# A hybrid two-layer model step: 48 instead of 32 latent tokens outside the dense expert products, 56 instead of 64 early blocks, index picks laid out anew

## The chip, the cores and the metric

The kernel runs on one core of a Trainium2 chip. Its engines work side by side, each through its own list of instructions in order: TensorE (PE; its weight loads are shown apart as PEld) multiplies matrices into PSUM, VectorE (DVE), ScalarE (ACT) and GpSimd (POOL) compute element by element, and SyncE (SP) issues transfers. The metric is the device time of one execution in microseconds (us); a time of a kernel is the median of several executions.

## The reference, cut to what matters

Two layers run over 640 tokens of 1024 features: 512 latent tokens and 128 context tokens. Each layer is a mixer (a gated convolution in layer 0, a state-space scan in layer 1) and then PEER, an expert layer with 16,384 experts of one neuron each. A token has 8 heads; each head scores two sets of 128 keys, keeps the top 16 of both, forms the sums, and keeps the best 16 pairs as experts:

```python
s1, i1 = lax.top_k(s[:, :, 0], PEER_TOPK)
s2, i2 = lax.top_k(s[:, :, 1], PEER_TOPK)
cand = (s1[..., :, None] + s2[..., None, :]).reshape(T, PEER_HEADS, PEER_TOPK * PEER_TOPK)
sc, pos = lax.top_k(cand, PEER_TOPK)
idx = jnp.take_along_axis(cidx, pos, axis=-1)
g = jax.nn.softmax(sc, axis=-1)
act = jnp.einsum('td,thkd->thk', tb, u[ib])
out = jnp.einsum('thk,thkd->td', jax.nn.gelu(act, approximate=False) * gb, v[ib])
```

So each token uses 128 of the experts: a dot product of the token with the expert's row of u, a GELU, a gate, and a weighted sum of rows of v.

## The kernel before, in words

PEER is computed in two ways. **Dense**: for `ND` = 480 latent tokens the kernel multiplies all 16,384 experts, in `NBLK` = 128 blocks of 128 experts. The first product (`u_blocks`, tile `pact`) takes a block's u against the tokens: 8 slices of features, each as three products (`mm3`, lines 125 to 127: high x high, low x high, high x low parts of a float32 number), 24 in all, each 128 x 128 weights against 480 columns. ScalarE applies GELU (tile `ga`). VectorE multiplies by the token's gates, which are zero for most experts (tile `h`, line 572), and splits the result into a high and a low part (line 581). The second product takes the block's v, again 8 x 3 products of 480 columns: six of eight feature slices sum up in PSUM (`acc`), two share a bank (`rot`) and are added to `sacc` by VectorE (line 641). Weights arrive as 512 KB tiles (`ur`, `wr`) on SP's queue; ScalarE makes their high part (line 89), VectorE the low part (`ul`, `wl`, line 98).

**Gathered**: the other 32 latent tokens (`NX`) and the 128 context tokens go another way. In a slot, GpSimd gathers one expert's row of u and v for each of 128 partitions (tile `uv`, 1 MB, three buffers, line 587), VectorE takes the dot with the token rows `hrow` (line 594), ScalarE applies GELU and the gate, and VectorE adds the weighted v row to `cacc` (line 604). The 32 latent tokens take four partitions each, so 32 slots serve them; 128 slots serve the context tokens, whose rows are loaded into `hrow` when the first group ends (`context_rows`). Then TensorE folds the four partial sums of a token with `quad` (`last_tokens`, line 616), into the bank `pact`.

Order in a layer: the norm also writes the token rows through TensorE transposes (`context_rows` in `peer_gates`); then come 16 key projections with scores, top-16 and `combine`, the picks of the second index, the gates spread to a table in DRAM by products of one-hot tiles (30 chunks of `TB` = 16 tokens, tile `pg`), and the main loop over the blocks. In the stages before the main loop, `fill` places steps of first products (three products, counted as 650 ns) between other work until `NSP` = 64 blocks are done; their activations wait in DRAM (`adram`). In the main loop the blocks that follow the early ones compute both products. `GATHER` says how many slots a block gets: 0.62 where it has only the second product, 1.95 where it has both. The order in the main loop is written out by hand; ahead of it a scheduler orders the instructions by their place in the code.

A pick (`pick`, lines 822 to 826) selects one of 16 values for each of 16 slots: a comparison makes a 16 x 16 mask (`cmp`), VectorE multiplies it with the values (line 825) and sums (line 826). It is done 8 times in `combine` (line 848) and 8 times in the pick stage (line 888) per layer.

Of the kernel before, what the change touches and what calls it, by code (L numbers as in the profile page):

```python
# [9 lines left out]
F32 = mybir.dt.float32  # L10
# [14 lines left out]
NX = 32  # L25
ND = NL - NX
NG = NX + P
KT = 8
# [4 lines left out]
NSP = 64  # L33
# [3 lines left out]
SG = 32  # L37
SW = 64
CH = 5
FILL_Q = (0, 9000)  # L40
GATHER = (0.62, 1.95)
# [5 lines left out]
FILL_T = 9000  # L47
FILL_G = 4800
# [65 lines left out]
class K:  # L114
# [28 lines left out]
    def run(s):  # L143
        nc, A = s.nc, s.A
        with ExitStack() as ctx:
# [9 lines left out]
            s.hdram = dram.tile([P, D], F32, name="hdram")  # L155
# [325 lines left out]
    def peer(s, i):  # L481
        nc, A = s.nc, s.A
        with ExitStack() as ctx:
# [52 lines left out]
            with ExitStack() as mc:  # L536
# [10 lines left out]
                xt = ap.tile([P, KT, NX], F32, name="xt")  # L547
                dg = ap.tile([P, NG], F32, name="dg")

                quad = ap.tile([P, NX], F32, name="quad")  # L550
                nc.vector.tensor_reduce(quad, s.ident.rearrange("p (q t) -> p t q", t=NX), axis=AX.X, op=ALU.add)
# [40 lines left out]
                def dot(n):  # L592
                    if n < NG:
                        nc.vector.scalar_tensor_tensor(UV[n][:, :D], UV[n][:, :D], 1.0, rows[n >= NX], op0=ALU.mult,  # L594
                                                       op1=ALU.mult, accum_out=dg[:, n:n + 1])
                        nc.scalar.activation(dg[:, n:n + 1], dg[:, n:n + 1], AF.Gelu)  # L596
                        nc.scalar.activation(dg[:, n:n + 1], dg[:, n:n + 1], AF.Copy, scale=cg[:, n:n + 1])

                def add_v(n):
                    t = UV.pop(n)  # L600
                    if n in (0, NX):
# [5 lines left out]
                def context_rows():  # L607

                    rows.append(hp.tile([P, D], F32, name="hrow"))
                    nc.sync.dma_start(rows[1], s.hdram)  # L610

                def last_tokens():

                    o = vps.tile([P, NL], F32, name="pact")[:, :KT * NX].rearrange("p (k t) -> p k t", t=NX)
                    for k in range(KT):
                        nc.tensor.matmul(o[:, k, :], cacc[:, k * P:(k + 1) * P], quad, start=True, stop=True)
                    nc.vector.tensor_tensor(xt, o, s.mod[i][:, 40:, 0:1].to_broadcast([P, KT, NX]), op=ALU.mult)
# [25 lines left out]
                for a in range(NBLK - 2):  # L643
# [27 lines left out]
                    while slot + due < NG and (credit >= 1 or a == NBLK - 3):  # L671
                        due, credit = due + 1, credit - 1
                    n0 = int(a + LAG >= NSP)
                    for n in range(max(due, 1)):
                        if n == 0 and n0 == 0:
                            add_rot(o, n6, a < 2)
                        if n < due:
# [4 lines left out]
                            if slot == NX - 1:  # L682
                                context_rows()
# [6 lines left out]
                    if before < NX <= slot:  # L690
                        assert a + LAG < NSP
                        last_tokens()
# [50 lines left out]
    def peer_gates(s, i, hi, lo, hrow, cidx, cgate, wq, fill, V, order):  # L743
        nc, A = s.nc, s.A
        with ExitStack() as pc:
# [6 lines left out]
            hctx = tk.tile([P, D], F32, name="hctx")  # L752
# [4 lines left out]
            def context_rows(k, t):  # L757

                if k % 4 == 0:
                    bank.append(qps.tile([P, 8, P], F32, name="pss", bufs=1))  # L760
                o = bank[-1]
                nc.tensor.transpose(o[:, k % 4, :], t[:, NL:], s.ident)
                four = tk.tile([P, P // NX, NX], F32, name="four", bufs=2)
                nc.gpsimd.tensor_copy(four, t[:, None, ND:NL].to_broadcast([P, P // NX, NX]))
                nc.tensor.transpose(o[:, 4 + k % 4, :], four.rearrange("p a b -> p (a b)"), s.ident)
                if k % 4 == 3:
                    for n, dst in ((0, hctx), (4, hrow)):
                        nc.scalar.activation(dst[:, (k - 3) * P:(k + 1) * P],
                                             o[:, n:n + 4].rearrange("p a b -> p (a b)"), AF.Copy)
                if k == KT - 1:  # L770
                    nc.scalar.dma_start(s.hdram, hctx)

            with ExitStack() as nx:
                s.norm(i, 1, hi, lo, s.pool(nx, "normtmp"), context_rows)
            s.close_x()

            stc = tk.tile([P, 16, 16], F16, name="stc")
            qc = tk.tile([P, 16, 16], F16, name="qc")
            for r in range(16):
                nc.gpsimd.memset(stc[:, r, :], float(STARTS[r]))  # L780
                nc.gpsimd.memset(qc[:, r, :], float(r))

            B16 = [P, CH, 16, 16]
            with qx:
# [37 lines left out]
                def pick(eq, vals, dst):  # L822

                    pr = qp.tile(B16, F16, name="pr")
                    nc.vector.tensor_tensor(pr, eq, vals[:, :, :, None].to_broadcast(B16), op=ALU.mult)  # L825
                    nc.vector.tensor_reduce(dst, pr.rearrange("p t r k -> p t k r"), axis=AX.X, op=ALU.add)

                def combine(h, a, b):
                    (v1, f1), (v2, _) = a, b
                    cd = qp.tile([P, CH, NCAND], F32, name="cd")  # L830
                    for p0, p1, nq, o in CAND:
# [9 lines left out]
                    pf = qp.tile([P, CH, 16], F16, name="pf")  # L841
                    nc.vector.tensor_copy(pf, pos)
# [4 lines left out]
                    cmp = qp.tile(B16, F16, name="cmp")  # L847
                    nc.vector.tensor_tensor(cmp, pf[:, :, None, :].to_broadcast(B16),
                                            stc[:, None].to_broadcast(B16), op=ALU.is_ge)
                    pick(cmp, d1, I1[:, :, h, :])  # L850
# [32 lines left out]
                for h in range(8):  # L883
                    fill(FILL_G)
                    q = qp.tile([P, CH, 16], F16, name="pf")
                    nc.vector.tensor_copy(q, PF[:, :, h, :])
                    eq = qp.tile(B16, F16, name="cmp")
                    nc.vector.tensor_tensor(eq, q[:, :, None, :].to_broadcast(B16),
# [562 lines left out]
```

## Time and profile before

| | us |
|---|---|
| median of three executions | 4118.25 (4109.04 to 4119.88) |
| the profiled execution | 4117.18 |
| its span in the trace | 4115.5 |
| TensorE busy | 4000.5 |
| VectorE busy | 3414.4 |
| ScalarE busy | 1661.4 |

The span runs from the first to the last instruction of the trace; the rest of the execution's time lies around it. Mean moved bytes are 233 GB/s over the span, and the mean granted clock of TensorE is 0.987 of full speed. In layer 0, PEER takes about 285 to 1866 us: scores to 492, picks to 586, one-hot chunks to 804, the rest of the early blocks to 846, blocks with the second product alone to 1163, blocks with both products to 1824, and the end. In layer 1 the same stages begin near 2524 us. A busy share is an average over stages, and an engine's idle time matters only where something waits for it.

### The profile page before, as it was taken

Reading aid. Unit: us, or ns where it says so; the run is one execution under the profiler, and the core shown is the slowest. Engines: PE = TensorE matmul, PEld = TensorE weight load, DVE = VectorE, ACT = ScalarE, POOL = GpSimd, SP = SyncE. Lnnn points to the kernel's source line nnn. Section 1 sums busy time; section 2 is a strip of 40 time slices with the busy share of each in tenths; the row PEclk is TensorE's granted clock in tenths of the full one; section 3 lists DMA queues with packets and bytes.
Section 4 is the critical chain, followed back from the end, with each engine's and each line's share of the span. In section 5 each row is a group of like instructions: output and inputs, shape, how many; then the busy total and the mean of one; then the engine's idle time right before and its main releaser. Section 6 shows DMA issues by size and latency. Waiting matters only on the chain.

```text
span 4115.5 us, 59000 instructions
## 1 busy us (share of the span) xinstructions
PE 4000.5 (97%) x22253; PEld 3543.9 (86%) x22253; DVE 3414.4 (83%) x6324; ACT 1661.4 (40%) x3060; POOL 421.6 (10%) x535
## 2 busy tenths in 40 slices
PE   8999999999999999999999999999999999999998
PEld 6999978788888888888999998987878888888887
DVE  7979997678788888878999867998858878888886
ACT  5233234433333333336555644223443333333332
POOL 0000000001111111111010100000001111111110
PEclk8999999999999999999999999999999999999999
DMA  6643238888888888963333234224888889998894
GB/s 218 219 159 109 81 131 248 266 307 321 313 316 324 322 322 322 327 249 123 118 102 119 85 128 148 94 86 161 249 280 300 323 316 325 323 323 321 323 324 181
DMA packets 344807, 957.33 MB, mean 233 GB/s; under 512 B 30091, under 2 KB 192139, under 8 KB 302537
## 3 DMA queue, kind: packets, MB, share of 16 engines
q1 hardware_dynamic: 147914, 514.53, 36.5%
q0 software_dynamic: 52224, 338.36, 22.1%
q10 hardware_dynamic: 144384, 100.67, 7.7%
q8 instruction: 174, 2.85, 0.3%
q14 instruction: 111, 0.91, 0.1%
HBM read 839.34 MB, written 114.04 MB: 232 GB/s over the span
## 4 chain that ended last, share of the span: by engine, by line
issue 41%; PE 32%; DVE 14%; POOL 8%; ACT 2%; DMA 2%; ACTq 1%; POOLq 0%; SPq 0%; DVEq 0%
POOL uv L587 8%; PE pact L125 3%; PE pact L126 3%; PE pact L127 3%; PE pj L125 2%; PE pj L126 2%; PE pj L127 2%; DVE ul L98 1%; DVE wl L98 1%; PE pg L978 1%; DMA uv<-uv,cidx 1%; PE pg L979 1%; DVE pr L825 1%; DVE idx L799 1%; DVE scr L795 1%
## 5 line engine op out<-in xcount | busy, mean ns | idle before, releaser
L125 PE MATMUL pact<-hnh,uh 128*128 128x480 f32 x2048 | 789.7, 386 | 12.7 <-ACT ga L508 9.4
L127 PE MATMUL pact<-hnh,ul 128*128 128x480 f32 x2048 | 781.7, 382 | 9.6 <-DVE ul L98 9.4
L126 PE MATMUL pact<-hnl,uh 128*128 128x480 f32 x2048 | 784.1, 383 | 0.0
L125 PE MATMUL acc<-h,wh 128*128 128x480 f32 x1536 | 584.6, 381 | 0.0
L127 PE MATMUL acc<-h,wl 128*128 128x480 f32 x1536 | 581.7, 379 | 0.0
L126 PE MATMUL acc<-h,wh 128*128 128x480 f32 x1536 | 581.7, 379 | 0.0
L89 ACT ACTIVATE wh<-wr 128x1024 fp32r<-128x1024 f32 x385 | 404.8, 1052 | 398.1 <-DMA wr<-uv 105.1
L98 DVE TENSOR_TENSOR wl<-wr,wh 128x1024 fp32r<-128x1024 f32 x385 | 469.7, 1220 | 59.4 <-ACT wh L89 58.3
L587 POOL DMA_INDIRECT uv<-uv,cidx x320 | 335.7, 1049 | 1661.8 <-DVE cacc L604 1540.1
L125 PEld LDWEIGHTS pact<-hnh,uh 128*128 128x128 f32 x2048 | 387.0, 189 | 76.1 <-ACT ga L508 13.1
L127 PEld LDWEIGHTS pact<-hnh,ul 128*128 128x128 f32 x2048 | 386.5, 189 | 74.0 <-DVE ul L98 13.6
L594 DVE SCALAR_TENSOR_TENSOR uv<-uv,hrow 128x1024 f32<-128x1024 f32 x320 | 390.8, 1221 | 57.3 <-DMA uv<-uv,cidx 55.6
L126 PEld LDWEIGHTS pact<-hnl,uh 128*128 128x128 f32 x2048 | 386.5, 189 | 58.3
L604 DVE SCALAR_TENSOR_TENSOR cacc<-uv,dg,cacc 128x1024 f32<-128x1024 f32 x316 | 405.1, 1282 | 0.0
L508 ACT ACTIVATE ga<-pact 128x480 f32<-128x480 f32 x256 | 145.6, 569 | 626.3 <-PE pact L127 626.0
L98 DVE TENSOR_TENSOR ul<-ur,uh 128x1024 fp32r<-128x1024 f32 x256 | 312.3, 1220 | 88.7 <-ACT uh L89 88.2
L89 ACT ACTIVATE uh<-ur 128x1024 fp32r<-128x1024 f32 x256 | 269.0, 1052 | 252.5 <-DMA ur<-uT 111.2
L581 DVE TENSOR_TENSOR h<-h,h 128x480 fp32r<-128x480 f32 x256 | 168.5, 658 | 197.0 <-PE rot L126 196.5
L127 PEld LDWEIGHTS acc<-h,wl 128*128 128x128 f32 x1536 | 289.1, 188 | 46.1
L126 PEld LDWEIGHTS acc<-h,wh 128*128 128x128 f32 x1536 | 289.1, 188 | 44.1
L125 PEld LDWEIGHTS acc<-h,wh 128*128 128x128 f32 x1536 | 289.4, 188 | 43.1
L596 ACT ACTIVATE dg<-dg 128x1 f32<-128x1 f32 x320 | 63.9, 200 | 422.3 <-DVE uv L594 422.3
(342 smaller groups left out, 8004.8 us busy)
## 6 DMA issues: line engine op xcount, KB each, us to landing
ur<-uT SPq DMA_DIRECT2D x256, 512.0 KB
wr<-uv SPq DMA_DIRECT2D x256, 512.0 KB
gdram<-st ACTq DMA_DIRECT2D x30, 2048.0 KB
gt<-gdram SPq DMA_DIRECT2D x62, 960.0 KB
mw<-ada_wT SPq DMA_DIRECT2D x80, 512.0 KB
adram<-ga ACTq DMA_DIRECT2D x128, 240.0 KB
ga<-adram SPq DMA_DIRECT2D x128, 240.0 KB
wr<-ssd_w SPq DMA_DIRECT2D x48, 512.0 KB
```

The lines of the kernel that those rows point to most:

```text
L89: s.K.nc.scalar.activation(hi.rearrange("p a b -> p (a b)"), s.raw[s.nh], AF.Copy)
L98: s.K.nc.vector.tensor_sub(lo.rearrange("p a b -> p (a b)"), s.raw.pop(s.ns), hi.rearrange("p a b -> p (a b)").bitcast(F32))
L125: mm(out, wh, mh, start=start, stop=False)
L126: mm(out, wh, ml, start=False, stop=False)
L127: mm(out, wl, mh, start=False, stop=stop)
L508: nc.scalar.activation(g, pa, AF.Gelu)
L581: nc.vector.tensor_sub(h2, h, h1.bitcast(F32))
L587: nc.gpsimd.indirect_dma_start(out=t[:], out_offset=None, in_=A["uv"].rearrange("l e d -> (l e) d"), in_offset=bass.IndirectOffsetOnAxis(a ...
L594: nc.vector.scalar_tensor_tensor(UV[n][:, :D], UV[n][:, :D], 1.0, rows[n >= NX], op0=ALU.mult, op1=ALU.mult, accum_out=dg[:, n:n + 1])
L596: nc.scalar.activation(dg[:, n:n + 1], dg[:, n:n + 1], AF.Gelu)
L604: nc.vector.scalar_tensor_tensor(cacc, t[:, D:], dg[:, n:n + 1], cacc, op0=ALU.mult, op1=ALU.add)
L795: nc.vector.match_replace(scr[:, t], v[:, t, :8], src[:, t], imm_value=-3e38)
```

## The change

`NX` becomes two groups, 16 and 32 tokens, so `ND` is 464: every dense product has 464 columns. The 16 tokens take eight partitions each, 16 slots; the layer has 176 slots instead of 160. `NSP` is 56. Token rows are made and loaded for three groups (two changes of `hrow` in the main loop, two foldings), and a block's slots do not run past a group's end. The picks compare pairs of neighbouring slots, with the values along the inner axis. The gate table is written in sub-chunks of 16 tokens, two to a transfer, and the last of the now 29 chunks alone. `FILL_Q`, `FILL_P` and `GATHER` set new amounts of fill and slots.

```diff
-NX = 32
-ND = NL - NX
-NG = NX + P
+NX = (16, 32)
+ND = NL - sum(NX)
+G0 = (0, NX[0], sum(NX))
+NG = sum(NX) + P
-NSP = 64
+NSP = 56
-SG = 32
+SG = 16
-FILL_Q = (0, 9000)
-GATHER = (0.62, 1.95)
+FILL_Q = (0, 7000)
+GATHER = (0.60, 1.98)
+FILL_P = 3200
...
-                def context_rows():
+                def next_rows(g):
                     rows.append(hp.tile([P, D], F32, name="hrow"))
-                    nc.sync.dma_start(rows[1], s.hdram)
+                    nc.sync.dma_start(rows[-1], s.hdram[g - 1])
-                def last_tokens():
+                def last_tokens(g):
+                    n = NX[g]
...
                     for k in range(KT):
-                        nc.tensor.matmul(o[:, k, :], cacc[:, k * P:(k + 1) * P], quad, start=True, stop=True)
+                        nc.tensor.matmul(o[:, k, :], cacc[:, k * P:(k + 1) * P], fold[g], start=True, stop=True)
...
-                    while slot + due < NG and (credit >= 1 or a == NBLK - 3):
+                    while slot + due < NG and (credit >= 1 or a == NBLK - 3) and not (due and slot + due in G0):
...
-                            if slot == NX - 1:
-                                context_rows()
+                            if slot + 1 in G0:
+                                next_rows(G0.index(slot + 1))
...
+                for g in range(3):
...
                     nc.tensor.transpose(o[:, k % 4, :], src, s.ident)
...
-                def pick(eq, vals, dst):
+                def pick(slots, marks, op, vals, dst):
+                    eq = qp.tile(B16, F16, name="cmp")
+                    pairs = [P, CH * 16, 8, 2]
+                    nc.vector.tensor_tensor(
+                        eq.rearrange("p t k (r b) -> p (t k) r b", b=2),
+                        slots.rearrange("p t k b -> p (t k) b")[:, :, None, :].to_broadcast(pairs),
+                        marks.rearrange("p (r b) -> p r b", b=2)[:, None].to_broadcast(pairs), op=op)
                     pr = qp.tile(B16, F16, name="pr")
-                    nc.vector.tensor_tensor(pr, eq, vals[:, :, :, None].to_broadcast(B16), op=ALU.mult)
-                    nc.vector.tensor_reduce(dst, pr.rearrange("p t r k -> p t k r"), axis=AX.X, op=ALU.add)
+                    nc.vector.tensor_tensor(pr, eq, vals[:, :, None, :].to_broadcast(B16), op=ALU.mult)
+                    nc.vector.tensor_reduce(dst, pr, axis=AX.X, op=ALU.add)
+                def twice(src):
+                    t = qp.tile([P, CH, 16, 2], F16, name="pf")
+                    nc.vector.tensor_copy(t, src[:, :, :, None].to_broadcast([P, CH, 16, 2]))
+                    return t
...
                 for h in range(8):
-                    fill(FILL_G)
...
+                    fill(FILL_P)
+                    pick(twice(PF[:, :, h, :]), qc, ALU.is_equal, F2[:, :, h, :], I2[:, :, h, :])
...
-                for n in range(P // NX):
-                    for dst, src in ((cidx, last), (cgate, fl(SC, 3))):
-                        nc.sync.dma_start(dst[n * NX:(n + 1) * NX, :NX], src[P - NX:, n * NX:(n + 1) * NX])
+                for g, m in enumerate(NX):
+                    p0 = P - NL + ND + G0[g]
+                    for n in range(P // m):
+                        for dst, src in ((cidx, last), (cgate, fl(SC, 3))):
+                            nc.sync.dma_start(dst[n * m:(n + 1) * m, G0[g]:G0[g] + m], src[p0:p0 + m, n * m:(n + 1) * m])
```

Three places in the order of instructions. First VectorE where the pick stage of layer 0 begins (`pf` the slots, `cmp` the mask, `pr` the products, `I` the picked index, `ul` a low part of weights); before:

```order
L886 COPY pf<-PF 128x80 x2
L888 TENSOR_TENSOR cmp<-pf,qc 128x1280 x2
L825 TENSOR_TENSOR pr<-cmp,F_2744 128x1280 x2
L826 TENSOR_REDUCE I_2741<-pr 128x5x16
L98 TENSOR_TENSOR ul<-ur,uh 128x1024
L826 TENSOR_REDUCE I_2741<-pr 128x5x16
L98 TENSOR_TENSOR ul<-ur,uh 128x1024
```

and now:

```order
L846 COPY pf<-PF 128x160 x2
L836 TENSOR_TENSOR cmp<-pf,qc 128x1280 x2
L841 TENSOR_TENSOR pr<-cmp,F_2744 128x1280 x2
L842 TENSOR_REDUCE I_2741<-pr 128x5x16 x2
L101 TENSOR_TENSOR ul<-ur,uh 128x1024
```

The copy of the slots has twice the elements, and one split of weights instead of two stands behind two picks, as less fill is asked for.

Second TensorE at the end of the block in which the group of 32 tokens ends (layer 0), before:

```order
L125 MATMUL rot<-h_10820,wh 128x480
L126 MATMUL rot<-h_10870,wh 128x480
L127 MATMUL rot<-h_10820,wl 128x480
L616 MATMUL pact<-quad,cacc 128x32 x8
L125 MATMUL rot<-h_10868,wh 128x480
L126 MATMUL rot<-h_10912,wh 128x480
```

and now, where it is block 61 instead of 51:

```order
L128 MATMUL rot<-h_11226,wh 128x464
L129 MATMUL rot<-h_11311,wh 128x464
L130 MATMUL rot<-h_11226,wl 128x464
L622 MATMUL pact<-fold_8134,cacc 128x32 x8
L128 MATMUL pact<-hnh,uh 128x464
L129 MATMUL pact<-hnl,uh 128x464
```

The folding products write the bank `pact`; behind them stands now the next block's first product, which uses the same bank. The group of 16 tokens ends at block 26, in the part where only second products run, as the old group did.

Third VectorE in the last block of layer 0's main loop and behind it, before (from `h` of block 125 on):

```order
L572 TENSOR_TENSOR h<-ga,gt 128x480
L581 TENSOR_TENSOR h_16659<-h,h_16592 128x480
L98 TENSOR_TENSOR wl<-wr,wh 128x1024
L641 TENSOR_TENSOR sacc<-sacc,rot 128x480
L581 TENSOR_TENSOR h_16691<-h,h_16657 128x480
L98 TENSOR_TENSOR wl<-wr,wh 128x1024
L724 TENSOR_TENSOR x<-x,xt 128x8x32
```

and now:

```order
L577 TENSOR_TENSOR h<-ga,gt 128x464
L586 TENSOR_TENSOR h_16738<-h,h_16659 128x464
L101 TENSOR_TENSOR wl<-wr,wh 128x1024
L599 SCALAR_TENSOR_TENSOR uv,dg<-uv,hrow 128x1024
L609 SCALAR_TENSOR_TENSOR cacc<-uv,dg,cacc 128x1024
L648 TENSOR_TENSOR sacc<-sacc,rot 128x464
L609 SCALAR_TENSOR_TENSOR cacc<-uv,dg,cacc 128x1024
L586 TENSOR_TENSOR h_16775<-h,h_16736 128x464
L101 TENSOR_TENSOR wl<-wr,wh 128x1024
L731 TENSOR_TENSOR x<-x,xt 128x8x48
```

A dot and two adds of gathered rows now stand ahead of the last split of v's weights (`wl`); before, no slot was left for the last two blocks.

## Rows read from the trace of the kernel before

**Rows 1.** The page, part 1: busy time, share, instructions.
```profile
PE 4000.5 (97%) x22253; PEld 3543.9 (86%) x22253; DVE 3414.4 (83%) x6324; ACT 1661.4 (40%) x3060; POOL 421.6 (10%) x535
```

**Rows 2.** Windows: stretch; PE, PEld, DVE, ACT, POOL busy; PEclk; DMA; GB/s.
```profile
300.00:492.00 192.00, 192.00 (x1194) 182.01 (x1194) 180.63 (x928) 63.34 (x111) 1.30 (x3) 1.00 0.29 97
492.00:586.00 94.00, 84.87 (x384) 70.17 (x382) 93.69 (x248) 26.53 (x36) 0.00 (x0) 0.98 0.32 110
1163.00:1824.00 661.00, 660.79 (x3056) 572.82 (x3055) 555.20 (x691) 248.34 (x501) 125.45 (x122) 1.00 0.89 322
```

**Rows 3.** Waits of DVE, 1163 to 1824 us: total, times, longest.
```profile
DVE h L581 <- PE rot L126: 47.7, 54, 3.1
...
DVE uv L594 <- DMA uv<-uv,cidx: 20.8, 27, 4.2
```

**Rows 4.** Timeline of PE: start, length; 480 columns, then 320.
```profile
1828.13 0.38 PE L125 MATMUL pact<-hnh,uh 128*128 128x480 f32 x1
...
1833.26 0.38 PE L125 MATMUL rot<-h,wh 128*128 128x480 f32 x1
...
99.79 0.31 PE L125 MATMUL cg<-chi,wh 128*128 128x320 f32 x1
...
102.14 0.31 PE L126 MATMUL cg<-clo,wh 128*128 128x320 f32 x1
```

**Rows 5.** Timeline of POOL: gathers of two blocks.
```profile
1411.35 1.11 POOL L587 DMA_INDIRECT uv<-uv,cidx  x1 [2.05 <-DVE cacc L604]
...
1432.20 1.11 POOL L587 DMA_INDIRECT uv<-uv,cidx  x1 [2.88 <-DVE cacc L604]
```

**Rows 6.** Groups of DVE by form: busy us, mean ns, idle before.
```profile
L98 DVE TENSOR_TENSOR ul<-ur,uh 128x1024 fp32r<-128x1024 f32 x256 | 312.3, 1220 | 88.7 <-ACT uh L89 88.2
L604 DVE SCALAR_TENSOR_TENSOR cacc<-uv,dg,cacc 128x1024 f32<-128x1024 f32 x316 | 405.1, 1282 | 0.0
L594 DVE SCALAR_TENSOR_TENSOR uv<-uv,hrow 128x1024 f32<-128x1024 f32 x320 | 390.8, 1221 | 57.3 <-DMA uv<-uv,cidx 55.6 <-issue 0.4
L826 DVE TENSOR_REDUCE I<-pr 128x80 f32<-128x1280 f16 x32 | 84.3, 2640 | 0.5
L825 DVE TENSOR_TENSOR pr<-cmp,F 128x1280 f16<-128x1280 f16 x16 | 23.3, 1485 | 0.0
L888 DVE TENSOR_TENSOR cmp<-pf,qc 128x1280 f16<-128x1280 f16 x16 | 12.7, 822 | 0.0
L897 DVE TENSOR_REDUCE smx<-ex 128x40 f32<-128x640 f32 x2 | 1.7, 826 | 0.0
```

**Rows 7.** Windows, columns as in Rows 2.
```profile
841.00:844.00 3.00, 3.00 (x16) 2.58 (x15) 1.62 (x2) 1.06 (x1) 0.00 (x0) 1.00 1.04 390
1126.00:1133.00 7.00, 7.00 (x27) 5.96 (x26) 3.83 (x7) 2.14 (x3) 0.00 (x0) 0.78 0.44 153
```

**Rows 8.** Timeline of PE: one token group of the gate products.
```profile
643.32 0.22 PE L978 MATMUL pg<-o,oh 128*128 128x128 f16 x1 [0.55 <-ACT st L981]
...
643.71 0.22 PE L979 MATMUL pg<-o,ol 128*128 128x128 f16 x1
```

**Rows 9.** Group of PE by line, 285 to 300 us.
```profile
L765 PE MATMUL pss<-ident,four 128*128 128x128 f32 x5 | 1.9, 372 | 0.0
```

**Rows 10.** Timeline of PE around the change of rows, layer 0.
```profile
1119.59 0.48 PE L125 MATMUL rot<-h,wh 128*128 128x480 f32 x1 [1.37 <-DVE sacc L641]
...
1121.93 3.31 PE L616 MATMUL pact<-quad,cacc 128*128 128x32 f32 x16 [1.42 <-DVE cacc L604]
```

**Rows 11.** Wait of PE, 3340 to 3410 us (layer 1).
```profile
PE pact L616 <- DVE cacc L604: 1.0, 1, 1.0
```

**Rows 12.** Timeline of SP: small copies of indices.
```profile
586.85 2.41 SPq L914 DMA_DIRECT2D cidx<-last  x4
```

**Rows 13.** Timeline of PE at the end of layer 0.
```profile
1845.55 0.49 PE L127 MATMUL rot<-h,wl 128*128 128x480 f32 x1 [0.64 <-DVE wl L98]
```

**Rows 14.** The page, part 5: a weight load.
```profile
L125 PEld LDWEIGHTS pact<-hnh,uh 128*128 128x128 f32 x2048 | 387.0, 189 | 76.1 <-ACT ga L508 13.1
```

More of the change, by code (lines that the diff above doesn't have):

```diff
@@ L546, in peer @@
                 cacc = ap.tile([P, D], F32, name="cacc")
-                xt = ap.tile([P, KT, NX], F32, name="xt")
+                xt = ap.tile([P, KT, NL - ND], F32, name="xt")
                 dg = ap.tile([P, NG], F32, name="dg")
-                quad = ap.tile([P, NX], F32, name="quad")
-                nc.vector.tensor_reduce(quad, s.ident.rearrange("p (q t) -> p t q", t=NX), axis=AX.X, op=ALU.add)
+                fold = []
+                for n in NX:
+                    fold.append(ap.tile([P, n], F32, name=f"fold{n}"))
+                    nc.vector.tensor_reduce(fold[-1], s.ident.rearrange("p (q t) -> p t q", t=n), axis=AX.X, op=ALU.add)
                 G, H, UV = {}, {}, {}
@@ L689, in peer @@
                     s.mm3(part, vh[:, 6 + n6, :], vl[:, 6 + n6, :], h1, h2, True, False)
-                    if before < NX <= slot:
-                        assert a + LAG < NSP
-                        last_tokens()
+                    if before < slot and slot in G0:
+                        last_tokens(G0.index(slot) - 1)
                     if a == NBLK - 8:
@@ L755, in peer_gates, with token_rows @@
             bank = []
-            def context_rows(k, t):
+            def token_rows(k, t):
                 if k % 4 == 0:
[L760 to L771, printed above, removed]
+                    bank[:] = [qps.tile([P, 8, P], F32, name="pss", bufs=1), qps.tile([P, 4, P], F32, name="psx", bufs=1)]
+                for g in range(3):
+                    o = bank[g // 2][:, 4 * (g % 2):4 * (g % 2) + 4]
+                    src = t[:, NL:]
+                    if g < 2:
+                        n, t0 = NX[g], ND + G0[g]
+                        some = tk.tile([P, P // n, n], F32, name=f"some{g}", bufs=2)
+                        nc.gpsimd.tensor_copy(some, t[:, None, t0:t0 + n].to_broadcast([P, P // n, n]))
+                        src = some.rearrange("p a b -> p (a b)")
+                    nc.tensor.transpose(o[:, k % 4, :], src, s.ident)
+                    if k % 4 == 3:
+                        nc.scalar.activation(hlat[g][:, (k - 3) * P:(k + 1) * P], o.rearrange("p a b -> p (a b)"), AF.Copy)
+                        if g and k == KT - 1:
+                            nc.scalar.dma_start(s.hdram[g - 1], hlat[g])
@@ L773, in peer_gates @@
             with ExitStack() as nx:
-                s.norm(i, 1, hi, lo, s.pool(nx, "normtmp"), context_rows)
+                tp = s.pool(nx, "normtmp")
+                hlat = [hrow] + [tp.tile([P, D], F32, name=f"hrows{n}") for n in range(2)]
+                s.norm(i, 1, hi, lo, tp, token_rows)
             s.close_x()
-            stc = tk.tile([P, 16, 16], F16, name="stc")
-            qc = tk.tile([P, 16, 16], F16, name="qc")
+            stc = tk.tile([P, 16], F16, name="stc")
+            qc = tk.tile([P, 16], F16, name="qc")
@@ L846, in combine @@
                     nc.vector.tensor_sub(d1[:, :, 1:], f1[:, :, 1:], f1[:, :, :15])
[L847 to L850, printed above, removed]
+                    pick(pf, stc, ALU.is_ge, d1, I1[:, :, h, :])
                 qs, sco = {}, {}
@@ L972, in peer_gates @@
                     o1, oh, ol = OH.pop(c)
-                    if c * TB % SG == 0:
-                        st = sp.tile([P, NBLK, SG], F32, name="st")
+                    if c % 2 == 0:
+                        st = sp.tile([P, NBLK // GA, 2, GA, SG], F32, name="st")
                     for t in range(0, TB, 4):
```

41 lines of the change are left out of this document (17 added, 24 removed).

## The prediction

> **What bounds the kernel now.** I read the page's first part, then a table of busy time by stage, then waits and single instructions where a number was wanted. The page says TensorE is busy for 97% of the span, VectorE 83% [rows 1]; that is an average, so the stages decide [rows 2]. From 1163 to 1824 us (layer 0, the blocks that compute both products) TensorE is busy 660.79 of 661 us, VectorE 555.20. Over those 661 us VectorE waits 47.7 us for TensorE to free a buffer, and 20.8 us for gathered rows [rows 3]: VectorE runs ahead and is held by TensorE. The stretch of layer 1 from 3403 us reads alike. From 300 to 492 us (scores and top-16) TensorE is busy throughout, VectorE 180.63 of 192. Only from 492 to 586 us (index picks) does it turn: VectorE 93.69 of 94 us, TensorE 84.87, and layer 1 repeats it at 2731 us. So TensorE's products set the time, but for some 9 us of idle TensorE per layer in the pick stage.
>
> **Dense products (the gain).** Each layer has 128 blocks of 24 + 24 products: 12,288 in all, now 480 columns wide, then 464. Their spacing: 24 first products lie between 1828.13 and 1833.26 us, 213.8 ns each; 16 products of 320 columns lie between 99.79 and 102.14 us, 146.9 ns each [rows 4]. That is 66.9 ns for 160 columns, 6.7 ns for 16. In the middle of the stage two blocks take 1432.20 - 1411.35 = 20.85 us (four gathers, two to a block) [rows 5], 217.2 ns a product; with that the slope gives 7.0 ns. I take 6.8 ns: 12,288 x 6.8 = **-83.6 us** (82.3 to 86.0). A block goes from 10.42 to 10.10 us.
>
> The Trainium skill, TensorE: Matmul & The Clock Gate, section Back-to-back issue gap, lets weight load and product together set the spacing of a stream and gives 81 ns at 128 columns and 131 ns at 512, 0.13 ns per column; by that 16 columns would be worth an estimated 2.1 ns, 26 us in all, and the sum would end near 4098. The rows at 320 and 480 columns show three times that slope, and I go by the rows.
>
> What must not become slower under it, per block of both products: VectorE has 555.20/661 x 10.42 = 8.75 us of work. It loses three operations' 16 columns (0.05 us) and gains 0.03 of a gathered slot (a dot and an add, 1.22 + 1.28 us [rows 6]: 0.08): 8.78 of 10.10 us. Its waits for gathered rows are now 20.8 us in 63 blocks, 0.33 us each. The transfers: weights 2 x 0.52 MB, gates 0.24, gathers 1.98 x 1.05 = 3.36 MB a block, 333 GB/s against 322 now [rows 2]; 390 GB/s has been moved for 3 us [rows 7]. I cost this at nothing: the cover is the 1.3 us per block in which VectorE would wait for TensorE. The 16 more slots per layer (2 x 16 x 2.5 = 80 us of VectorE) lie in that cover too, as there are 73 such blocks per layer instead of 65.
>
> **Early blocks, 56 instead of 64.** 8 x 24 products per layer move from the gate stages to the main loop; as TensorE is full in both, the move itself is 0. What it does to the pick stage stands next.
>
> **Picks.** The multiply reads its 16 values along the inner axis instead of repeating one: 1485 ns to the 822 ns of the compare of the same size, which already reads so [rows 6]. The sum reads neighbours instead of every 16th: now 2640 ns for 1280 elements, 2.06 ns each, while the sum over contiguous float32 takes 826 ns for 640 and the dot 1221 for 1024 (1.03 ns per element between them), so 826 + 640 x 1.03 = 1485 ns. Doubling the compared slots adds 80 elements, 0.09 us. Net -1.72 us a pick.
> The Trainium skill, SBUF — State Buffer, section Door 1: The DMA port swizzle, says that full bandwidth needs at least two hits per 16-byte line. The old sum strides 32 bytes and so hits each line once, which agrees with two cycles an element; the trace has no float16 sum of neighbours, so no row shows that contiguity cures it.
> Ends: the sum keeps 2640 ns, or runs at the compare's 822. I take 1485, because the contiguous sum is the nearest row.
> In the pick stage VectorE loses 9 picks (15.5 us) and the weight splits of 14,800/650 = 23 fewer fill steps (2.9 blocks, 1.22 us each [rows 6]: 3.5): 19 us. TensorE loses 23 x 3 products (14.7 us, done later instead) and 2.5 us of narrower ones: 17.2. Idle TensorE falls by 1.8 us a layer: **-4 us**. If the sum stays at 2640, VectorE loses 8.7 us only, TensorE idles 8.5 us more here and, as VectorE falls behind the shortened fill in the eight score steps (0.57 + 0.45 us less VectorE against 2.3 us less TensorE each, from 94% busy), some 5 more there: +27 for both layers. At 822 ns: -15.
>
> **Gate chunks.** 29 instead of 30 chunks of 16 tokens: 2 x 32 products at (643.71 - 643.32)/7 = 56 ns [rows 8]: **-4 us**. Reordering the tile changes neither the size of a copy nor the 512-byte runs; the odd last chunk writes 256-byte runs, and lands before the 34 us of remaining fill are over.
>
> **Second gathered group.** Eight more transposes a layer, 372 ns at most [rows 9], two more copies of 0.6 us on ScalarE and eight small folding products, in a stretch where both engines are in the chain: **+4 us** (2 to 9).
> One more change of token rows per layer, with its folding products. In layer 0 the one there is cost TensorE 1.4 + 1.4 us of waiting for VectorE [rows 10], and then 1126 to 1133 us ran at a granted clock of 0.78, part of it at the lower level of 1.2 GHz [rows 7]; in layer 1 only 1.0 us [rows 11]. The new one falls in a block whose successor needs the very bank that the folds fill, so a VectorE multiply lies between two blocks. Its row load is requested one block ahead. 2.5 us each: **+5 us** (1 to 14).
>
> **Small copies.** 24 instead of 8 on SP per layer, 0.6 us each (four took 2.41 [rows 12]); weight loads queue behind them, ScalarE's high parts behind those. The loads are two tiles ahead and the stage has VectorE as its bound: **+2 us** (0 to 19).
>
> **End of the layer.** Slots now run to the very last block. In block 125 TensorE needs 24 x 0.21 = 5 us, and asks for the last block's low part five products later, at 6.1. VectorE does a low part of the gated activations (0.6 by the same 1.03 ns per element), a weight split (1.2 [rows 6]), a dot and an add (2.5), a partial sum (0.6), the last add (1.2), and then low part and split of the last block (1.8): 7.9 us. It waits 0.64 us for it now [rows 13], then 1.8 plus what the clock loses: **+3 us** for both layers (2 to 10).
>
> **Sum.** The profiled execution took 4117.2 us (span 4115.5), 1.1 below the median of the three. 4117.2 - 83.6 - 4 - 4 + 4 + 5 + 2 + 3 = 4039.6: **4040 us**.
>
> **Rivals.**
> (a) The sum over picks gains nothing. Against it: contiguous sums at one element per cycle. Price +31 against mine: 4071.
> (b) Transfers bind in the main loop. Were the 322 GB/s of that stretch a ceiling, a block would take 3.36/0.322 = 10.43 us, 0.33 over, in 146 blocks: +48, 4088. Against it: the 390 GB/s, and that the rate there is what TensorE's pace asks for.
> (c) Row changes, copies and tail at their upper ends: 4060 to 4078: a wait of TensorE at each of the four row changes like the one in layer 0, the weight loads late by all sixteen more copies, and a full slot's 2.5 us and its clock loss at each layer's end. For it: each happens once now; against it: the loads two tiles ahead.
> (d) The products' spacing does not shrink with 16 columns, being set by weight loads: the dense term falls away, 4123. Loads take 189 ns [rows 14], below 207, and at 320 columns they overlap within a spacing of 147; so hardly. The skill's rule above points this way.
> (e) Slower: gathers come late for three buffers. A gather is asked for when an add frees its buffer, and its dot comes about 7.5 us later; if gathers slip, VectorE (8.78 us of work, in order) stalls with the weight splits behind it, and TensorE waits for these. It decides once waits pass 1.3 us a block. For a loss of 0.3% the block must reach 10.10 + (4130 - 4040)/146 = 10.7 us, 1.9 us of waits, six times what the trace shows. At 2.1 us: 4160.
>
> **Numbers.** Chances: mine 0.68 (4022 to 4058 from its bounds), (a) 0.10, (b) 0.04, (c) 0.09, (d) 0.03, (e) 0.06. The range 4016 to 4072 takes in mine, (a) and most of (c), and leaves out some 0.15. Three runs spread by 0.26%, so 0.3%, 12 us, is what can be told from no change: faster is below 4106. Faster: mine, (a), (b), (c) = 0.91; same: (d) = 0.03; slower: (e) = 0.06.
>
> **What would show it.** Spacing of the first products 207 ns and block period 10.1 us; TensorE without waits in the blocks of both products, VectorE's waits there still mostly for TensorE; the sum of a pick near 1.49 us, its multiply 0.82; the pick stage some 19 us shorter with TensorE still idle there; four row changes of a few us; TensorE's wait for the last low part under 3 us. Wrong if dots wait for gathers over 1.3 us a block, if the pick's sum stays at 2.6 us, or if a stall of tens of us stands at the row changes or behind the small copies.

## Result and profile after

| | median us | lowest to highest | runs |
|---|---|---|---|
| before, same chip | 4119.07 | 4109.04 to 4122.51 | 4 |
| changed | 4074.24 | 4067.70 to 4083.35 | 4 |

The ratio is 0.9899, 95% interval 0.9879 to 0.9919: faster, by 45 us where 77 were forecast, and 2 us outside the range. The profiled execution took 4074.67 us (span 4072.6). The page, part 1 [rows 1]:

```profile
PE 3935.5 (97%) x22237; PEld 3560.5 (87%) x22237; DVE 3404.3 (84%) x6416; ACT 1667.5 (41%) x3120; POOL 455.5 (11%) x583
```

The shares tell nothing new. The windows by stage do (layer 0: scores, picks, gates, blocks of both products; columns as in [rows 2]):

```profile
300.00:475.00 175.00, 174.38 (x1120) 168.46 (x1120) 161.20 (x894) 58.36 (x105) 2.31 (x5) 1.00 0.28 96
475.00:555.00 80.00, 71.34 (x331) 61.74 (x330) 79.66 (x277) 23.73 (x33) 0.00 (x0) 0.96 0.35 116
555.00:796.00 241.00, 230.08 (x1734) 200.35 (x1733) 174.64 (x157) 114.46 (x188) 3.61 (x4) 0.97 0.82 253
1135.00:1796.00 661.00, 657.63 (x3119) 585.87 (x3118) 567.14 (x713) 253.33 (x518) 130.34 (x129) 1.00 0.90 333
```

Two stages are not as forecast. In the last, TensorE is idle for 3.4 us (0.2 before), and what VectorE waits for has turned round. Its waits there, for [rows 3]:

```profile
DVE uv L599 <- DMA uv<-uv,cidx: 54.6, 48, 5.5
DVE h L586 <- PE rot L129: 17.3, 29, 0.7
DVE sacc L648 <- PE rot L130: 14.1, 26, 0.9
```

Before, it waited 47.7 us and, in the row below, 36.5 us for TensorE, and 20.8 for gathered rows; now the gathers lead.

```profile
DVE sacc L641 <- PE rot L127: 36.5, 52, 1.9
```

One wait for gathered rows, first in VectorE's timeline, then in TensorE's, then the window behind it:

```profile
1757.79 1.22 DVE L101 TENSOR_TENSOR ul<-ur,uh 128x1024 fp32r<-128x1024 f32 x1
1764.48 1.22 DVE L599 SCALAR_TENSOR_TENSOR uv<-uv,hrow 128x1024 f32<-128x1024 f32 x1 [5.46 <-DMA uv<-uv,cidx]
...
1766.83 0.63 DVE L648 TENSOR_TENSOR sacc<-sacc,rot 128x464 f32<-128x464 f32 x1
```
```profile
1765.36 0.37 PE L130 MATMUL acc<-h,wl 128*128 128x464 f32 x1
1767.51 0.48 PE L128 MATMUL rot<-h,wh 128*128 128x464 f32 x1 [1.78 <-DVE sacc L648]
...
1768.47 0.59 PE L129 MATMUL pact<-hnl,uh 128*128 128x464 f32 x1
1768.86 0.59 PE L130 MATMUL pact<-hnh,ul 128*128 128x464 f32 x1
1769.24 0.59 PE L128 MATMUL pact<-hnh,uh 128*128 128x464 f32 x1
```
```profile
1768.00:1772.00 4.00, 4.00 (x13) 3.46 (x13) 3.79 (x6) 2.48 (x5) 1.20 (x2) 0.57 0.79 271
```

VectorE stands 5.46 us before a dot; the partial sum queued behind it is late; TensorE stands 1.78 us; and then its products start 390 ns apart instead of 210, as the granted clock, 0.57 on average over the 4 us behind, is for most of them at its lower level (1.2 GHz). Not every wait is followed by that: behind one of 2.94 us at 3991.55 us the products come 210 ns apart at once. In sum it about doubles the waits: in the two main loops TensorE is idle for 25 us, and waits and slowed products together take 46.

In the gate stage the wait has another cause. ScalarE (ACTq is its DMA issue), then TensorE, then the window behind it:

```profile
757.57 2.67 ACTq L998 DMA_DIRECT2D gdram<-st  x1
760.28 5.55 ACTq L513 DMA_DIRECT2D adram<-ga  x1
765.94 1.06 ACT L92 ACTIVATE uh<-ur 128x1024 fp32r<-128x1024 f32 x1 [7.95 <-issue]
```
```profile
761.62 0.38 PE L130 MATMUL pact<-hnh,ul 128*128 128x464 f32 x1
767.04 0.76 PE L128 MATMUL pact<-hnh,uh 128*128 128x464 f32 x1 [5.04 <-ACT uh L92]
```
```profile
768.00:772.00 4.00, 3.88 (x11) 3.26 (x11) 1.47 (x2) 0.96 (x1) 3.09 (x4) 0.53 0.82 246
```

The store of the odd 29th chunk comes 5 us behind that of the pair before it. Its issue, 0.38 us for every other gate store, holds ScalarE for 2.67 us, that of the activation store behind it for 5.55, and the weight split that TensorE needs is queued behind both. Layer 1 repeats it (2.29 and 5.30 us of ScalarE, 4.4 us of TensorE). The kernel before has such holds too: of 28 activation stores within 8 us behind a gate store, 27 take over 0.5 us to issue, up to 7.34. What the change adds is the odd store, where TensorE waits for it.

Stage lengths from TensorE's timeline (bounds: last product of the key projections, first transpose of the gates, first product into an accumulator, last one), layer 0 / layer 1, us. The profiled execution of the old picks is the slowest of its ten, 15 us above their median.

| kernel | picks | gates | main loop |
|---|---|---|---|
| before | 98.6 / 98.5 | 255.9 / 257.5 | 1013.0 / 1010.7 |
| changed | 79.5 / 79.5 | 240.9 / 242.7 | 1037.8 / 1037.4 |
| changed, second time | 77.9 / 78.0 | 243.4 / 243.7 | 1036.0 / 1039.7 |
| single store first | 77.9 / 79.5 | 247.0 / 248.1 | 1030.7 / 1039.2 |
| single store on SP | 79.5 / 79.5 | 237.8 / 237.0 | 1035.3 / 1039.8 |
| half gathers | 79.5 / 78.0 | 241.0 / 244.1 | 1023.3 / 1024.0 |
| add first | 77.9 / 79.5 | 241.8 / 240.8 | 1029.5 / 1029.6 |
| GpSimd's stores | 79.5 / 79.5 | 238.1 / 236.7 | 1043.6 / 1042.2 |
| old picks | 96.0 / 96.4 | 251.2 / 251.4 | 1040.4 / 1046.1 |
| more fill | 84.1 / 83.9 | 232.2 / 233.5 | 1039.6 / 1043.7 |
| before, add first | 98.4 / 98.4 | 255.4 / 257.9 | 1013.7 / 1013.8 |
| add first, SP | 79.5 / 79.5 | 237.9 / 238.1 | 1028.9 / 1027.0 |

What TensorE loses in these stages, both layers together, us: by how much the spacing of its products exceeds the median for products of their shape, summed where that is over 40 ns. It takes in waits and slowed products.

| kernel | picks | gates | main loop | sum |
|---|---|---|---|---|
| before | 29.6 | 32.8 | 23.2 | 85.6 |
| changed | 27.3 | 45.8 | 45.6 | 118.7 |
| single store on SP | 27.1 | 37.0 | 45.4 | 109.5 |
| add first | 25.7 | 44.9 | 29.6 | 100.2 |
| add first, SP | 27.2 | 38.3 | 26.5 | 92.0 |

The change adds 33 us of such loss, about what is missing: 13 in the gates, 22 in the main loop.

### The profile page after: what moved, and what is told of

It reads as the page before. It is cut to its first block, busy times and chain, and to the rows that moved or that the text cites. A ratio compares the mean times of both kernels' runs of the same rounds, so it can differ in the third digit from the quotient of the medians.

```text
span 4072.6 us, 59158 instructions
## 1 busy us (share of the span) xinstructions
PE 3935.5 (97%) x22237; PEld 3560.5 (87%) x22237; DVE 3404.3 (84%) x6416; ACT 1667.5 (41%) x3120; POOL 455.5 (11%) x583
## 4 chain that ended last, share of the span: by engine, by line
issue 40%; PE 36%; DVE 10%; POOL 8%; DMA 3%; ACT 2%; ACTq 1%; POOLq 0%; SPq 0%; DVEq 0%
POOL uv L592 8%; PE pact L128 3%; PE pact L130 3%; PE pact L129 3%; PE pj L128 2%; PE pj L129 2%; PE pj L130 2%; DMA uv<-uv,cidx 1%; PE pq L130 1%; PE pq L129 1%; PE pq L128 1%; PE pg L992 1%; PE pg L993 1%; DVE wl L101 1%; PE bank L128 1%
## 5 line engine op out<-in xcount | busy, mean ns | idle before, releaser
L128 PE MATMUL pact<-hnh,uh 128*128 128x464 f32 x2048 | 781.8, 382 | 18.0 <-ACT uh L92 14.6
L130 PE MATMUL pact<-hnh,ul 128*128 128x464 f32 x2048 | 773.6, 378 | 15.5 <-DVE ul L101 15.2
L129 PE MATMUL pact<-hnl,uh 128*128 128x464 f32 x2048 | 773.3, 378 | 0.0
L128 PE MATMUL acc<-h,wh 128*128 128x464 f32 x1536 | 574.7, 374 | 0.0
L130 PE MATMUL acc<-h,wl 128*128 128x464 f32 x1536 | 574.5, 374 | 0.0
L129 PE MATMUL acc<-h,wh 128*128 128x464 f32 x1536 | 572.6, 373 | 0.0
L592 POOL DMA_INDIRECT uv<-uv,cidx x352 | 363.5, 1033 | 1712.6 <-DVE cacc L609 1572.1
L599 DVE SCALAR_TENSOR_TENSOR uv<-uv,hrow 128x1024 f32<-128x1024 f32 x352 | 429.8, 1221 | 130.9 <-DMA uv<-uv,cidx 128.5
L128 PEld LDWEIGHTS pact<-hnh,uh 128*128 128x128 f32 x2048 | 391.1, 191 | 65.2 <-ACT uh L92 16.2
L609 DVE SCALAR_TENSOR_TENSOR cacc<-uv,dg,cacc 128x1024 f32<-128x1024 f32 x346 | 443.1, 1281 | 0.0
L511 ACT ACTIVATE ga<-pact 128x464 f32<-128x464 f32 x256 | 142.1, 555 | 583.3 <-PE pact L130 583.3
L586 DVE TENSOR_TENSOR h<-h,h 128x464 fp32r<-128x464 f32 x256 | 163.5, 639 | 127.2 <-PE rot L129 124.4
```

What stands on the lines that cost most here:

```text
L128: mm(out, wh, mh, start=start, stop=False)
L129: mm(out, wh, ml, start=False, stop=False)
L130: mm(out, wl, mh, start=False, stop=stop)
L511: nc.scalar.activation(g, pa, AF.Gelu)
L586: nc.vector.tensor_sub(h2, h, h1.bitcast(F32))
L592: nc.gpsimd.indirect_dma_start(out=t[:], out_offset=None, in_=A["uv"].rearrange("l e d -> (l e) d"), in_offset=bass.IndirectOffsetOnAxis(a ...
```

## Experiments

The theory: late gathers (C) and ScalarE held in issuing stores (A) took what was missing. All ratios are to the kernel before on the same chip; the runs lay on two chips, so differences are taken between ratios.

**Base.** The changed kernel, unedited.

> The changed kernel once more, beside the others of this call, as their base. Every theory: 0.990 of the kernel before, within 0.002.

4070.67 us, ratio 0.9897 (0.9880 to 0.9915), as the first time.

**Half gathers.**

```diff
-                            out=t[:], out_offset=None, in_=A["uv"].rearrange("l e d -> (l e) d"),
+                            out=t[:, :D], out_offset=None, in_=A["uv"].rearrange("l e (b d) -> (l e b) d", b=2),
...
-                        nc.vector.scalar_tensor_tensor(cacc, t[:, D:], dg[:, n:n + 1], cacc,
+                        nc.vector.scalar_tensor_tensor(cacc, t[:, :D], dg[:, n:n + 1], cacc,
```

> Each gathered slot brings 1024 of the 2048 elements, and the sum reads the same half as the dot: half of the experts' data for the gathered tokens is left out; no engine's work changes. Theory C (late gathers block VectorE, and behind it the partial sums that TensorE waits for, some 8 to 10 us a layer with the clock that is lost behind each wait): VectorE's waits for gathered rows fall from 60 us a layer to under 15, and the time by 14 to 22 us, to about 4055. Rival D (TensorE's waits in the main loop come from the row changes and VectorE's order of work): 4068 to 4075 us.

4048.53 us, 0.9818 (0.9802 to 0.9833), 33 us under the changed kernel (0.9897 - 0.9818 = 0.0079 of 4119); the main loop alone is 14 us shorter per layer. VectorE's waits, 1135 to 1796 us, are as before again:

```profile
DVE h L586 <- PE rot L129: 41.3, 58, 3.0
DVE sacc L648 <- PE rot L130: 35.7, 58, 0.9
DVE uv L599 <- DMA uv<-uv,cidx: 7.3, 5, 3.6
```

The time fell by more than C said, the waits as it said; D falls. This run relieves the transfers too, so it doesn't say whether late starts or bandwidth made the gathers late.

**Add first.** Same bytes, only an earlier start.

```diff
-                            dot(slot + 1)
                             add_v(slot)
+                            dot(slot + 1)
```

> The add of a slot goes ahead of the dot of the next, so that a buffer is free and the next gather asked for some 1.2 us earlier, with the same traffic. Theory C (gathers are late because three buffers let them start late): VectorE's waits for gathered rows fall to half or less, the time by 8 to 18 us, to about 4060. Rival E (transfers at 334 GB/s have no more to give: a gather that starts earlier lands no earlier): waits as before, 4070 to 4076 us. Against both: the add may now wait for ScalarE's two small operations on the dot just before it (0.7 us where 0.63 us of other work lies between); if that counts, slower than the changed kernel by up to 5 us.

4053.40 us, 0.9833 (0.9821 to 0.9846): 26 us under the changed kernel, and its five runs lie within 2.6 us of each other where the changed kernel's four spread over 15.7. The same waits, and the windows of the stretch:

```profile
DVE h L586 <- PE rot L129: 36.6, 53, 3.0
DVE sacc L648 <- PE rot L130: 30.6, 49, 0.9
DVE uv L599 <- DMA uv<-uv,cidx: 10.5, 13, 3.9
```
```profile
1135.00:1796.00 661.00, 660.29 (x3149) 589.65 (x3148) 571.55 (x715) 248.99 (x517) 208.71 (x130) 1.00 0.93 334
```

334 GB/s against 333 with the waits: transfers were no ceiling (E falls). The gathers started too late. The feared wait of the add for ScalarE is 0.6 us in this stretch. Of the 26 us, 16 lie in the main loops of the profiled runs.

The edit does more than start a gather 1.2 us earlier. From a gather's start on GpSimd to the moment when VectorE is free for its dot, the median in the stretch is 7.0 us in the changed kernel (7.7 before) and 9.7 here: the request comes a dot (1.2 us) earlier, and the dot that needs it an add (1.3 us) later. And in the changed kernel the add that frees a buffer stands behind the dot that waits: the buffer whose dot began at 1752.45 us was added, and so free, only behind the late dot of 1764.48, and the next gather came late in turn. VectorE's and GpSimd's timelines, changed kernel:

```profile
1752.45 1.22 DVE L599 SCALAR_TENSOR_TENSOR uv<-uv,hrow 128x1024 f32<-128x1024 f32 x1
...
1765.63 1.28 DVE L609 SCALAR_TENSOR_TENSOR cacc<-uv,dg,cacc 128x1024 f32<-128x1024 f32 x1
```
```profile
1755.15 1.09 POOL L592 DMA_INDIRECT uv<-uv,cidx  x1 [2.41 <-DVE cacc L609]
1767.18 0.94 POOL L592 DMA_INDIRECT uv<-uv,cidx  x1 [10.94 <-DVE cacc L609]
```

**The same edit in the kernel before.**

> The add ahead of the next dot, in the kernel before. Theory C (the lateness of gathers is what the change adds: 1.98 slots per block in blocks 0.3 us shorter): the kernel before gains little, 0 to 8 us, against some 20 us that the same edit is worth in the changed one. Rival H (gathers were as late before, and the swap is worth the same to any version): 15 to 25 us less than the kernel before.

4115.89 us, 1.0001 (0.9989 to 1.0012). VectorE's wait for gathers, 20.8 us from 1163 to 1824 us without the edit [rows 3], falls there as well, and buys nothing:

```profile
DVE uv L594 <- DMA uv<-uv,cidx: 4.2, 4, 3.1
```

The median from a gather's start to a free VectorE is 10.1 us here, 7.7 without the edit. Before, these waits were covered; the change uncovered them. H falls.

**Single store first.** 1 + 14 pairs instead of 14 pairs + 1.

```diff
-                    if c % 2 or c == ND // TB - 1:
-                        n = c % 2 + 1
+                    if c % 2 == 0:
+                        n = 2 if c else 1
```

> The 29 gate chunks are stored one first, then 28 in pairs, so that a single chunk's store no longer stands right behind a pair's. Theory A (in the changed kernel the single store at the end and the store behind it hold ScalarE's queue for 2.7 + 5.5 us, the next weight split waits for ScalarE, and TensorE loses 5.2 us and some 2.8 us more at the lower clock, in each layer): 14 to 17 us less than the changed kernel, about 4059 us, and TensorE's wait near 762 us gone. Rival B (the weight loads are late there, or the gates are what TensorE waits for): the wait stays or moves, 4070 to 4075 us.

4080.04 us, 0.9893 (0.9876 to 0.9909): nothing gained. The wait at 762 us is gone, as A said, but its gain is not. Pairs now end just ahead of an activation store; ScalarE's timeline, then TensorE's:

```profile
735.29 0.38 ACTq L998 DMA_DIRECT2D gdram<-st  x1
735.74 5.31 ACTq L513 DMA_DIRECT2D adram<-ga  x1
```
```profile
742.75 0.26 PE L992 MATMUL pg<-o,oh 128*128 128x128 f16 x1 [5.75 <-ACT st L994]
```

The wait moved, which was B's sign; but what TensorE waits for here is ScalarE, held in issuing. So A named the mechanism and was wrong on the gain: any store issued within some 6 us behind a 2 MB one holds ScalarE, and where the two fall decides who waits.

**Single store on SP.**

```diff
-                        nc.scalar.dma_start(
+                        (nc.scalar if n == 2 else nc.sync).dma_start(
```

> The single store stays last, but SP issues it. Theory A (it is ScalarE's time in issuing that costs, not the store's traffic): 8 to 16 us less than the changed kernel, as ScalarE is free for the weight split; the store of activations behind it may still take 2 to 3 us. Rival B (the traffic delays the weight loads): no less than 4070 us, TensorE waits at the same place for the load.

4060.54 us, 0.9846 (0.9831 to 0.9862): 21 us under the changed kernel, beyond what A said. TensorE's wait for ScalarE's split falls from 5.0 to 0.6 us between 730 and 796 us; B falls. The gate stage's loss falls by 9 us for both layers. The stage table shows only 3 to 7 us per layer, and the runs differ by 14 us among themselves, so 7 to 21 us is what can be said.

**Activation stores by GpSimd.**

```diff
-                        nc.scalar.dma_start(s.adram[a], g)
+                        nc.gpsimd.dma_start(s.adram[a], g)
```

> GpSimd issues the stores of the early blocks' activations instead of ScalarE. Theory A (the issue behind a gate store holds ScalarE for 1 to 6 us, 14 times a layer, and TensorE waits behind that, for the weight splits and for the banks that ScalarE empties; the single last store is only the worst of them, and putting it first moved the wait): TensorE's idle time in the gate stage falls from about 30 us to under 18 in each layer, the time by 15 to 30 us. Rival B (VectorE's one-hot products and the weight loads set that stage, ScalarE's holding is cover): the gate stage keeps its 241 us and the time stays within 5 us of the changed kernel.

4077.36 us, 0.9911 (0.9895 to 0.9927): nothing gained. ScalarE is held by the odd gate store alone (0.84 and 1.95 us), and the gate stage is 3 to 7 us shorter, less than A said and more than B. It is given back at once: the first gather now stands on GpSimd behind these stores, and starts at 792.46 us where it started at 768.82. VectorE's timeline:

```profile
799.67 1.22 DVE L599 SCALAR_TENSOR_TENSOR uv<-uv,hrow 128x1024 f32<-128x1024 f32 x1 [6.14 <-DMA uv<-uv,cidx]
```

TensorE's first wait in the main loop is 8.2 us, 2.5 in the changed kernel. So this run doesn't decide what the holds of the other 14 stores cost.

**Old picks.** The layout of the picks alone undone (the compare, its constants and the copy of the slots likewise).

```diff
-                    nc.vector.tensor_tensor(pr, eq, vals[:, :, None, :].to_broadcast(B16), op=ALU.mult)
-                    nc.vector.tensor_reduce(dst, pr, axis=AX.X, op=ALU.add)
+                    nc.vector.tensor_tensor(pr, eq, vals[:, :, :, None].to_broadcast(B16), op=ALU.mult)
+                    nc.vector.tensor_reduce(dst, pr.rearrange("p t r k -> p t k r"), axis=AX.X, op=ALU.add)
```

> The changed kernel with the picks of indices laid out as before (compare, multiply and sum over the strided axis); all else as changed, the smaller fill between picks too. By the changed kernel's trace the new layout takes 1.7 us off a pick (multiply 817 ns, sum 1479 ns). Theory I (VectorE sets the pick stage, so its time there comes back in full): 15.5 us longer per layer in that stage and some more in the scores, 30 to 40 us more than the changed kernel, 0.997 to 1.000 of the kernel before. Rival J (the products not done there are done elsewhere, TensorE being the bound over the whole layer): 0 to 10 us more.

4122.62 us, 1.0005 (0.9996 to 1.0015): 44 us above the changed kernel, as theory I said and a little more; J falls. Groups of VectorE in its pick stage, and TensorE's waits for the weight splits that VectorE is late with (7.6 us in the changed kernel, second time):

```profile
L839 DVE TENSOR_REDUCE I<-pr 128x80 f32<-128x1280 f16 x10 | 25.6, 2591 | 0.0
L838 DVE TENSOR_TENSOR pr<-cmp,F 128x1280 f16<-128x1280 f16 x8 | 11.7, 1492 | 0.0
```
```profile
PE pact L130 <- DVE ul L101: 18.9, 5, 10.2
```

Without the new layout the rest of the change is worth nothing. That the smaller fill between picks needs the shorter picks fits TensorE's waits; no run has the old fill with the old picks.

**More fill between picks.** `FILL_P` 4400 instead of 3200.

> The number that sets how many early products go between two index picks is 4400 instead of 3200: 6.8 instead of 4.9 steps of three products per pick, taken from the end of the gate stage. Theory F (in the pick stage TensorE idles 13.6 us a layer because it is given 3.2 us of products per pick and VectorE takes some 4.2 us for one): TensorE's idle time there falls below 5 us and the time by 12 to 20 us. Rival G (VectorE sets that stage, and more products bring it more weight splits; the gate stage, with fewer products left over, then idles as much more): within 5 us of the changed kernel.

4063.46 us, 0.9868 (0.9852 to 0.9883): 12 us less by the ratio, though its interval overlaps the base's, and the profiled run, the slowest of four, shows only 4 to 5 us in picks and gates together. F's direction holds, its size doesn't; what TensorE loses in the picks (waits and slowed products) falls from 12 to 13.6 us to 8.7, not below 5. G falls too: the gate stage's loss, 47.0 us for both layers, is no larger than in the base (49.4).

**Mends together.** Add first and SP's single store; then with `FILL_P` 4400; then with the residual loaded in four parts:

```diff
-                        nc.sync.dma_start(s.x, s.xdram)
+                    if a >= NBLK - 8 and a < NBLK - 4:
+                        k = 2 * (a - NBLK + 8)
+                        nc.sync.dma_start(s.x[:, k:k + 2], s.xdram[:, k:k + 2])
```

> Two mends of the changed kernel together: the add ahead of the next dot, and the single last store issued by SP. If the two waits are separate, they add: 0.9833 less 0.003 to 0.005, some 0.979 of the kernel before, which is what was forecast for the change (0.981) or a little less. If one wait only gives way to the other: 0.983 or more.

> As the run with two mends, and 4400 instead of 3200 for the products between picks. If TensorE's idle time there is worth what its own run showed (0.003): 0.975 to 0.977 of the kernel before.

> As the run before, and the 2.6 MB of the residual that are loaded eight blocks ahead of a layer's end come in four parts, a block apart, so that the gathers of that block don't wait behind them (TensorE's wait near 1765 us in the changed kernel, 3.6 us with the clock). Theory: 0 to 6 us less than without it. Rival: the last parts land late for the sums at the end: up to 10 us more.

4044.53 us, 0.9813 (0.9800 to 0.9827); 4037.59 us, 0.9796 (0.9782 to 0.9810); 4035.81 us, 0.9795 (0.9781 to 0.9808). The first two mends are worth 0.0084, 35 us, together, less than the 47 of both alone (0.0064 and 0.0051): neither a plain sum nor one in place of the other. They bring the change to the ratio that was forecast (4040 / 4117.2 = 0.9812). `FILL_P` adds some 7 us, within the noise, and the parts of the residual nothing that can be measured, though VectorE's waits for gathers beside that load fall from 4.3 us to none (1730 to 1815 us) and from 4.7 to 1.5 (3930 to 4020). All three beat both kernels.

## Why the prediction was wrong

It was right that the kernel gets faster, and wrong by some 34 us in its size.

**The step that failed** is "I cost this at nothing: the cover is the 1.3 us per block". It set an average wait for gathers against an average cover. The average stayed below its bound (65.7 us from 803 to 1826 us, 0.9 us for each of 73 blocks, against 1.3), so the prediction's own sign of being wrong did not show. But TensorE feels single waits. Of a lone wait of 5.46 us it felt 1.78 (above), of one of 6.62 us 2.94, 3.68 less both times; one of 3.22 us at 1418.84 cost it nothing:

```profile
3988.51 1.23 DVE L599 SCALAR_TENSOR_TENSOR uv<-uv,hrow 128x1024 f32<-128x1024 f32 x1 [6.62 <-DMA uv<-uv,cidx]
```
```profile
3991.55 0.47 PE L128 MATMUL rot<-h,wh 128*128 128x464 f32 x1 [2.94 <-DVE sacc L648]
```

So VectorE's lead here is 3.7 us; what goes beyond it passes on. Waits close behind each other seem to share that lead: 3.99 us at 3401.03 was followed by 1.93 us of TensorE nine us later. Before, two waits were over 4 us, and of both TensorE felt 0.95. What passed, with the clock, makes most of the 22 us more that the main loops lose. Rival (e), with its threshold as an average and 0.06, had the mechanism and the wrong rule (by its own sum its price at 2.1 us is 4154, not 4160). Removing the lateness was worth 26 us, none of it in the kernel before.

**A second step** is "the odd last chunk ... lands before the 34 us of remaining fill are over". It looked at where the data lands, not at the engine that issues. That engine was held 8.2 us, and the fill itself needed it. Worth 7 to 21 us; 8 on top of the first mend. Of the 13 us that the gate stages lose more, it makes 9; the other 4 stay open.

The profiled runs add up: products without waits -82, gate chunks -4, TensorE's losses over the whole kernel +44 (33 in the three stages, the rest mostly ahead of layer 0's scores and at its end) make -42, and 4117.2 became 4074.7. That the two mends land on the forecast is in part luck: with both, TensorE still loses 13 us more than before, about the 14 that the prediction had added for its small terms, but not where it had put them.

The other terms, for both layers, from TensorE's timeline:
- Dense products -83.6: -82; products without waits start 217.0 ns apart before and 210.3 now. In an undisturbed stretch of GpSimd's timeline [rows 5] four gathers, two blocks, take 1734.92 - 1714.79 = 20.13 us, 209.7 ns a product where 209 to 210 was meant:

```profile
1714.79 1.09 POOL L592 DMA_INDIRECT uv<-uv,cidx  x1 [2.31 <-DVE cacc L609]
...
1734.92 1.09 POOL L592 DMA_INDIRECT uv<-uv,cidx  x1 [2.68 <-DVE cacc L609]
```

Rival (d) falls, and with it, for these products, the slope of the stream figures in the Trainium skill's TensorE: Matmul & The Clock Gate, Back-to-back issue gap.
- Picks -4: about -2 of TensorE's waits and slowed products. The stage is 19.1 us shorter where 19 was meant. The sizes were right, 1478 ns for 1485 and 817 for 822 [rows 6], so rival (a) falls:

```profile
L842 DVE TENSOR_REDUCE I<-pr 128x80 f32<-128x1280 f16 x10 | 14.6, 1478 | 0.0
L841 DVE TENSOR_TENSOR pr<-cmp,F 128x1280 f16<-128x1280 f16 x8 | 6.4, 817 | 0.0
```

The line rule of the Trainium skill's SBUF — State Buffer, Door 1: The DMA port swizzle, agrees: neighbours cured the float16 sum.
- Row changes +5: about 0. What TensorE loses from 8 us ahead of the folding products to 16 us behind them comes to 2.7 and 4.5 us in the two layers, for two changes each, against 5.9 and 1.2 before for one each [rows 10, 11]. The second group's +4 was not measured alone.
- Small copies +2: TensorE's waits from 520 to 600 us are 3.7 us, for low parts from VectorE, which waited 2.7 us for high parts there; so little can stand behind the copies. Gate chunks -4: as many products fewer as counted.
- End of the layer +3: TensorE's wait for the last low part, forecast at 1.8 us and more, was 0.7; the stretch from the last accumulator product to the next layer's first projection (in layer 1 to TensorE's last product) took 18.9 and 16.2 us in two runs (14.2 before) in layer 0, and 4.9 and 5.4 (5.1) in layer 1. So +2 to +5, mostly from the clock: the 30 small products of the norm take 6.50 and 4.24 us there, 3.46 before.
- Rival (b): 333 GB/s ran, and the add first, at 334 without the waits, shows that it was not the bound.

## What to carry to other kernels

A wait that is covered on average is not covered: set its longest cases, and those that come close together, against the lead that the waiting engine has, and add what the clock takes where it drops behind a wait of TensorE. Look at what stands in order behind a wait: here the add that frees the buffer for the next gather. Cost a store by the time that its issuing engine is held, not only by when it lands, and ask what that engine has queued behind it. An edit that moves two streams against each other may move such a wait instead of removing it.

## What the hardware showed unexpectedly

Issuing a store takes ScalarE 0.33 us for activations and 0.38 us for gates, but 0.9 to 5.6 us for every activation store within some 6 us behind a gate store (27 in the changed kernel; such a gate store is 2 MB in 512-byte runs, but for the odd one; up to 7.3 in the kernel before). The engine does nothing else meanwhile. One activation store 7.0 us behind takes 0.33. Why the issue is held was not settled.

Why a gather lands after 5 us in one block and 12 in another is settled only for the longest waits: they lie beside the load of the residual (issued at 1749.33 us), and four parts of it, with the add first, all but removed them, without a gain in time.
